# A two-layer conv / recurrence / pooling backbone: layer two's modulation as halves in the blockwise projection, and loads, casts and the norm's mean in another order

## The chip, the cores and the metric

The kernel runs on one core of one Trainium2 chip. Its time is device microseconds, lower is better. An instruction stream runs on each engine: PE (TensorE: matmuls; PEld is its weight load), DVE (VectorE), ACT (ScalarE), POOL (GpSimd) and SP (SyncE, which here only issues DMAs). Each takes its instructions in order and waits on semaphores for the others.

## The reference

One sequence of 1024 latent tokens with 1024 features (D), and 256 context tokens, pass two layers. Layer one (even) has a convolution branch and a recurrence branch side by side; layer two (odd) a pooling mixer.

```python
for l in range(2):
    shift, scale, gate = split(silu(c) @ mod_w[l] + mod_b[l], 3)
    h = rmsnorm(x, norm_g[l]) * (1 + scale) + shift
    if l == 0:
        va, vg, ga, xb, gb = split(h @ w_in, 5)
        u = depthwise_conv(va * sigmoid(vg), conv_w, conv_b)        # 31 taps
        y_a = silu(layernorm(u, ln_g, ln_b)) * silu(ga)
        y_b = rglru(shortconv(xb), h_ctx) * silu(gb)                # two directions, scan over tokens
        out = concat([y_a, y_b]) @ w_out
    else:
        u, g = split(h @ w_in2)                                     # 2048 each
        out = (einsum(pool(u), w_grp) * od_scale * silu(g)) @ w_out2
    x = x + gate * out
return rmsnorm(x, final_g)
```

The modulation of layer two (shift and scale, 16 columns of 128) needs only `c`, so it can be made at any time before layer two. Layer two's w_in and w_grp are multiplied beforehand in the kernel (the "folds").

## The kernel before

Features lie on the 128 partitions, tokens on the free axis, in row tiles of 128 and halves of 512 tokens. A float32 product is made of three matmuls: high part by high part, low by high, high by low. A weight is therefore loaded (wr), cast on ACT to its high part (wh) and subtracted on DVE or POOL to its low part (wl).

The stages in order:

1. Layer one's modulation, norm and two of the four folds, to about 104 us. Six whole rows of layer two's modulation are made here too (`mod_row_in`, L725).
2. A loop over eight feature tiles (xb, vg, va, then the recurrence's gates). DVE does the 31-tap convolution as a queue of small instructions; `fill(n)` issues the next n of them. For five tiles the sum of even and odd tokens is made ahead (`spread_sum`, into cL). The product gb follows, to about 520 us.
3. ga as four quads (`quad_fixed`: seven block products instead of eight, in banks qa, qb and qc), to 603.70 us. `cp_ga` copies a bank within a quad on ACT.
4. The blockwise projection of y_b, "wob": eight outputs of 48 matmuls (two halves of 24). Around it runs the layernorm of the convolution branch: `ln_mean` (matmul with ones), `ln_square` (subtract on DVE, square on ACT), `ln_add`, `ln_root` (matmul ms_ln of the sum lnsum, root on ACT), `ln_scale`, `ln_silu`, `ga_mult`. `wob_evict` takes a result out of PSUM by ACT (wo) and adds it on POOL (xp), or does both on DVE (m > 4). `raw_load`/`raw_split` bring a weight. `mod_half(0, n)` makes ten halves of modulation columns at m = 0.
5. The quads of y_a's projection, "woa", to about 795 us. Each product's bank is added to the residual tile x1 by DVE (L1498), and `mods` is stepped after each quad: the other ten halves. Then the two last folds run, to 839 us, and DVE scales x1 for layer two (L1547).
6. Layer two's quads v and g, pooling, the last projection and the final norm.

Up to the end of wob the order on every engine is the order of the program text: `on(engine, ...)` chains each instruction to the one before it. From there on a scheduler orders the instructions when the program is built. Every load goes through SP's queue, in its order, and waits there for a free buffer. Tiles of half width (lsq, wo, mod) share six buffers (`ttile`).

Of the kernel before, what the change touches and what calls it, by code (L numbers as in the profile page):

```python
# [49 lines left out]


NROW = 6
# [5 lines left out]
def body(ctx, tc, xT, ctxT, cc, ccol, modT, modW, win, gw, wout, wu, grp, wg, wo1, small, edge, ident, outT):  # L58
# [239 lines left out]
    rpool = tc.alloc_tile_pool(name="rpool", bufs=3)  # L298
# [3 lines left out]
    cL = cpool.tile([P, D], F32, name="cL")  # L302
    hh, hl, ch, cl = [], [], [], []
    with ExitStack() as sctx:
# [118 lines left out]
        def ctx_scale():  # L423
            rstd(accc, eps_r, "c")
            for i in range(2):
                v = cx[i].rearrange("p (k n) -> p k n", n=C)
                last["vec"] = nc.vector.tensor_tensor(out=v, in0=v, in1=accc.unsqueeze(1).to_broadcast([P, 4, C]),
                                                      op=mult)
# [45 lines left out]
        begin, chain[0] = chain[0], None  # L474
# [76 lines left out]

    def conv(j):
        acc_, late = banks(f"conv{j}", 0)
        ue, uo = us[j][:, 0::2], us[j][:, 1::2]
        ub = uo if j >= NSPREAD else both_sum(j)
# [3 lines left out]
        vec(nc.vector.tensor_scalar, out=acc_, in0=ue, scalar1=w(15), scalar2=None, op0=mult)  # L559
        yield  # L560
        vec(nc.vector.tensor_scalar, out=late, in0=uo, scalar1=w(16), scalar2=None, op0=mult)
        yield
        for n in range(NT + 1):
            if n < NT - 1 and n != 7:
                tap(acc_, ue, w(2 * n + 1), n - 7)
                yield
            if n != 8:
                tap(late, uo, w(2 * n), n - 8)
                yield
        if ub is uo:  # L570
# [23 lines left out]
    ended, summed, spread_ = [0], [1], [0]  # L594
    NSPREAD = 5

# [43 lines left out]
    with ExitStack() as actx:  # L640
# [91 lines left out]
        vec(nc.vector.tensor_tensor, out=m1[:, 0, :NROW], in0=m1[:, 0, :NROW], in1=col(O_MB + 3 * KT, NROW), op=add)  # L732
# [5 lines left out]
        for j in range(KT):  # L738
# [81 lines left out]
            fill(19 if state is None else 5 if final else 8)  # L820
# [54 lines left out]
        def gr_split(j):  # L875
            gws[j] = raw_split(grs.pop(j), f"gb{j}")
# [8 lines left out]
    rpool.release()  # L885
# [7 lines left out]
    m1p = hpool.tile([P, 2 * KT - NROW, 2], F32, name="m1p")  # L893
# [186 lines left out]
    def quad_weights(src, name):  # L1080
        raw = []
        for i in range(2):
            raw.append(wpool.tile([P, D], F32, tag="wr", name=f"wr_{name}_{i}"))
            sp(raw[i], src[i])
        a11, a12 = [raw[0][:, h] for h in HALF]
# [10 lines left out]

        yield op(a11, 1)
# [30 lines left out]
    def quad_fixed(name, keep, step):  # L1128
# [8 lines left out]
        for n, (ps, op, first) in enumerate(((a, "b11", True), (c, "t1", True), (b, "t2", False), (a, "b21", False),  # L1137
# [19 lines left out]
            pull()  # L1157
# [14 lines left out]

    def yr_step(n):
        if 0 < n < KT - 1:
            for h in range(2):
                yr_load(n + 1, h)
# [24 lines left out]
    block_sum(1)  # L1201
    gb_silu(4)
    gr_split(6)
    yr_step(1)
    block_split(1)
    gb_product(5, gws[5])
    block_sum(2)
    yr_step(2)
    block_split(2)
    block_sum(3)  # L1210
    gb_silu(5)
    gr_split(7)
    gb_product(6, gws[6])
    pull()
    yr_step(3)
# [3 lines left out]
    pull()  # L1219
# [27 lines left out]
    def mid_step(n):  # L1247
        fill(4)
# [7 lines left out]
    def wob_split(m):  # L1256
        if m < KT:
            gws[KT + m] = raw_split(obs.pop(m), f"wob{m}", vadd if m > 5 else gp)

    def last_step(n):  # L1260
# [11 lines left out]
        if n in (3, 5):  # L1272
            wob_split(n // 2 - 1)
            wob_load(n // 2 + 1)
# [10 lines left out]
    def xp_load(m, h):  # L1285
        if m < KT:
            xps[m, h] = vtile(f"xp{m}_{h}")
            sp(xps[m, h], xT[m][:, HALF[h]])

# [13 lines left out]

    lnmu, lnsq = {}, {}

    def ln_mean(h):
        lnmu[h], lnsq[h] = banks(f"mu{h}", h)
        on("pe", nc.tensor.matmul, lnmu[h], ones, lnacc[h][:, :H], start=True, stop=True)
# [748 lines left out]
```

## Time and profile before

| | us |
|---|---|
| median of 3 runs | 1334.56 (1333.38 to 1336.40) |
| profiled execution | 1333.44 |
| span of its instructions | 1331.6 |
| PE busy | 1274.4 (96%) |
| DVE busy | 1175.9 (88%) |
| ACT busy | 651.1 (49%) |
| POOL busy | 383.8 (29%) |
| mean granted clock of PE | 0.986 |

A row of the timeline gives start and duration in us, the engine, the line, output<-inputs and their shapes; in brackets the idle time before it and what ended it. Lines of the changed kernel are numbered differently from L725 on; helper calls all carry one line (L481 before, L477 after), so they are told apart by the names of tiles.

### The profile page before, as it was taken

The page shows a single profiled execution, that of the slowest core. Times are in us where ns is not written, and L with a number is a line of the kernel's source. Part 1 is how long each engine was busy: PE and PEld are TensorE (multiplying, and loading weights), DVE is VectorE, ACT ScalarE, POOL GpSimd, SP SyncE. Part 2 cuts the span into 40 slices and gives each one's busy share as a digit, 9 for nine tenths or more (in the row PEclk, how much of TensorE's full clock was granted, in tenths as well). Part 3 has the DMA queues.
Part 4 walks back from the last instruction along what each step waited for, and adds up shares of the span by engine and source line. Part 5 has one row for each costly group of instructions (what it writes and reads, how often), then busy time and mean ns, then how long its engine had stood idle before and what let it go on. Part 6 is the DMA issues. An engine that isn't in the chain of part 4 may idle for free. (4 is left out here: it accounts for less than half of the span.)

```text
span 1331.6 us, 15798 instructions
## 1 busy us (share of the span) xinstructions
PE 1274.4 (96%) x5552; PEld 1018.0 (76%) x5552; DVE 1175.9 (88%) x1780; ACT 651.1 (49%) x949; POOL 383.8 (29%) x207
## 2 busy tenths in 40 slices
PE   8989999999999999999699999999999999989995
PEld 3458888888888887777477877788778888778784
DVE  7988999999999998996999778998999987876875
ACT  5333656666656623353754336734333334634542
POOL 3064555675657615673320023000000000000002
PEclk9999999999999999999899999999999999999998
DMA  9975111121112174468466457244333334868613
GB/s 357 392 256 182 49 41 55 56 72 40 64 43 69 64 265 165 140 212 282 148 199 206 162 168 238 79 150 150 112 112 118 111 119 139 300 208 276 231 64 126
DMA packets 91218, 206.96 MB, mean 155 GB/s; under 512 B 8706, under 2 KB 28546, under 8 KB 91140
## 3 DMA queue, kind: packets, MB, share of 16 engines
q1 hardware_dynamic: 79236, 193.38, 42.8%
q10 hardware_dynamic: 11904, 12.59, 2.8%
q8 instruction: 43, 0.70, 0.2%
q14 instruction: 35, 0.29, 0.1%
HBM read 149.31 MB, written 56.62 MB: 155 GB/s over the span
## 5 line engine op out<-in xcount | busy, mean ns | idle before, releaser
L481 DVE SCALAR_TENSOR_TENSOR conv<-u,sm,conv 128x505 f32<-128x505 f32 (+6 forms) x224 | 152.6, 744 | 1.0
L1877 POOL TENSOR_TENSOR o<-x,rr 128x256 f32<-128x256 f32 (+1 forms) x9 | 8.0, 926 | 458.1 <-ACT rr L1865 455.2
L481 POOL TENSOR_TENSOR l<-l,l 128x1280 f32<-128x1280 f32 (+1 forms) x23 | 64.0, 2797 | 91.7 <-DVE l L481 65.5
L481 ACT ACTIVATE l<-g,sm 128x512 f32<-128x512 f32 (+1 forms) x96 | 58.6, 618 | 57.8 <-PE g L481 56.0
L285 PE MATMUL fold<-graw,wu 128*128 128x512 f32 x128 | 57.9, 613 | 2.7 <-DMA wu<-wu 2.7
L107 POOL TENSOR_TENSOR wl_wu<-wr_wu,wh_wu 128x1024 fp32r<-128x1024 f32 x8 | 19.3, 2410 | 122.4 <-ACT wh_wu L106 122.4
L481 PE MATMUL wob<-ybh,wl_wob 128*128 128x512 f32 x128 | 50.3, 393 | 1.7 <-POOL wl_wob L481 1.0
L481 PE MATMUL wob<-ybh,wh_wob 128*128 128x512 f32 x128 | 51.9, 405 | 0.0
L285 PEld LDWEIGHTS fold<-graw,wu 128*128 128x128 f32 x128 | 25.0, 197 | 34.9 <-issue 29.8
L481 PE MATMUL gb<-h0h,wl_gb 128*128 128x512 f32 x128 | 49.9, 390 | 1.5 <-POOL wl_gb L481 1.5
L106 ACT CAST wq_v<-wr_v 128x512 fp32r<-128x512 f32 x48 | 28.1, 620 | 46.2 <-DMA wr_v<-wfold 15.2
L481 PE MATMUL wob<-ybl,wh_wob 128*128 128x512 f32 x128 | 50.3, 393 | 0.0
L481 PE MATMUL vg<-h0h,wl_vg 128*128 128x512 f32 x128 | 50.0, 390 | 0.0
L481 PE MATMUL gb<-h0h,wh_gb 128*128 128x512 f32 x128 | 49.8, 389 | 0.0
L481 PE MATMUL gb<-h0l,wh_gb 128*128 128x512 f32 x128 | 49.8, 389 | 0.0
L481 PE MATMUL vg<-h0h,wh_vg 128*128 128x512 f32 x128 | 49.8, 389 | 0.0
L481 PE MATMUL vg<-h0l,wh_vg 128*128 128x512 f32 x128 | 49.8, 389 | 0.0
L481 PE MATMUL va<-h0h,wh_va 128*128 128x512 f32 x128 | 49.8, 389 | 0.0
L481 PE MATMUL va<-h0l,wh_va 128*128 128x512 f32 x128 | 49.8, 389 | 0.0
L481 PE MATMUL va<-h0h,wl_va 128*128 128x512 f32 x128 | 49.8, 389 | 0.0
L481 DVE TENSOR_TENSOR_SCAN l<-l,l 128x256 f32<-128x256 f32 (+1 forms) x32 | 48.7, 1521 | 1.1
L106 ACT CAST wq_g<-wr_g 128x512 fp32r<-128x512 f32 x48 | 28.3, 620 | 41.8 <-DVE wr_g L972 12.5
(697 smaller groups left out, 4393.6 us busy)
## 6 DMA issues: line engine op xcount, KB each, us to landing
mod<-modT SPq DMA_DIRECT2D x20, 512.0 KB, 7.4
x_part<-xp SPq DMA_DIRECT2D x32, 256.0 KB, 3.8
wr_v<-wfold SPq DMA_DIRECT2D x16, 512.0 KB, 4.0
wr_g<-wg SPq DMA_DIRECT2D x16, 512.0 KB, 4.7
wr_wo<-wo SPq DMA_DIRECT2D x16, 512.0 KB, 4.3
y_b<-y SPq DMA_DIRECT2D x24, 256.0 KB, 3.2
y_t<-y SPq DMA_DIRECT2D x24, 256.0 KB, 3.3
yr_t<-y_t SPq DMA_DIRECT2D x12, 512.0 KB, 5.9
```

Of the source, the lines that this page charges most:

```text
L106: return (nc.scalar.copy(hi, src), eng.tensor_tensor(out=lo, in0=src, in1=hi.bitcast(F32), op=sub))
L107: eng.tensor_tensor(out=lo, in0=src, in1=hi.bitcast(F32), op=sub))
L285: nc.tensor.matmul(ps, w[:, kc], gs[i], start=(i == 0), stop=(i == 3))
L481: last[eng] = f(*args, **kw)
L1877: nc.gpsimd.tensor_tensor(out=o[:, k - k0], in0=v, in1=rr, op=mult)
```

## The change

It has five parts.

- **Modulation of layer two.** The six whole rows at the start and the ten first halves at wob's m = 0 go away. All sixteen columns are made as two halves each in `mod_halves`, 32 steps, taken 4, 10, 9 and 9 after the four quads of woa (3, 3, 2 and 2 of ten steps before).
- **Convolution.** For the first six tiles two taps are computed on ACT (`conv_heads`), so that the first two DVE instructions add them in and two later taps fall away. The sums of `spread_sum` are made on POOL instead of DVE. `fill` counts change: 10 for 8 in the loop, 3 for 4 in the middle quads, none at wob's m = 0.
- **The layernorm in wob.** The convolution is ended before wob. The mean is taken after three of eight k-steps of output 0 instead of after output 0. Squares move from m = 1 to m = 0, roots to m = 1 and 2 (h = 0), scales and silus by one step.
- **Splits and loads.** gb's splits 5 to 7 go from POOL to DVE, wob's splits of 0, 1 and 5 too. Outputs' weights are loaded three ahead instead of four; the layer's x is loaded before the last quad ends.
- **Quads of ga.** `quad_weights` yields more often and is pulled by a table (1, 1, 1, 2, 1, 2, 1), so that instructions of the next quad's weights fall between others.

```diff
-        with tc.issue_after(begin.ins):
-            for n in range(NROW):
-                mod_row_in(rpool.tile([P, D], F32, tag="r", name=f"row{n}"), modT[1, n], m1[:, 0, n : n + 1])
...
+    def conv_heads(j):
+        for t, v, k in ((heads[0], us[j][:, 0::2], 17), (heads[1], us[j][:, 1::2], 18)):
+            act(t[:, : H - 1], v[:, 1:], AF.Identity, scale=col(O_CONVW + 31 * j + k))
+        headed[0] = j + 1
...
-        vec(nc.vector.tensor_tensor, out=cL[:, HALF[j % 2]], in0=us[j][:, 1::2], in1=us[j][:, 0::2], op=add)
+        gp(out=cL[:, HALF[j % 2]], in0=us[j][:, 1::2], in1=us[j][:, 0::2], op=add)
...
-            fill(19 if state is None else 5 if final else 8)
+            fill(19 if state is None else 5 if final else 10)
...
-            gws[j] = raw_split(grs.pop(j), f"gb{j}")
+            gws[j] = raw_split(grs.pop(j), f"gb{j}", vadd)
...
-            pull()
+            pull((1, 1, 1, 2, 1, 2, 1)[n])
...
-            gws[KT + m] = raw_split(obs.pop(m), f"wob{m}", vadd if m > 5 else gp)
+            gws[KT + m] = raw_split(obs.pop(m), f"wob{m}", gp if 1 < m < 5 else vadd)
...
     def mod_halves():
+        for n in range(2 * KT):
+            mod_half(0, n)
+            yield
         load_c(0, cH, HALF[1])
-        for n in range(NROW, 2 * KT):
+        for n in range(2 * KT):
...
         if m == 0:
-            for _ in range(KT - 1):
+            for k in range(KT - 1):
                 for h in range(2):
                     next(steps[h])
+                if k == 2:
+                    for h in range(2):
+                        ln_mean(h)
         for h in range(2):
             all_of(steps[h])
-            if m == MEAN + 1:
+            if m == 0:
                 for j in range(KT):
                     ln_square(j, h)
...
+            if h == 0 and m in (1, 2):
+                ln_root(m - 1)
+            if m == 2 and h == 0:
+                ln_scale(0)
...
-            if m == 0:
-                if h == 0:
-                    half_c(0)
-                for n in range(NROW + 5 * h, NROW + 5 * h + 5):
-                    mod_half(0, n)
         wob_split(m + 2)
-        wob_load(m + 4)
+        wob_load(m + 3)
...
-        for _ in range((3, 3, 2, 2)[m // 2]):
+        for _ in range((4, 10, 9, 9)[m // 2]):
             next(mods)
```

How the order on the engines changes is shown at three places. First ACT in ga, where the first quad ends and the second quad's weights begin (o00 a finished block, cp the copied bank, wq a weight's cast). Before:

```order
L481 ACTIVATE o00_ga0_4173<-qa_ga0_4086 128x512
L481 DMA ga_raw0_93<-o00_ga0_4173 128x512
L481 CAST wq_ga2q_1_4183<-wr_ga2q_0_4176 128x512
L481 COPY cp_ga0_4204<-qb_ga0_4088 128x512
L481 CAST wq_ga2q_5_4207<-wr_ga2q_1_4178 128x512
```

and now:

```order
L477 ACTIVATE o00_ga0_4183<-qa_ga0_4095 128x512
L477 DMA ga_raw0_93<-o00_ga0_4183 128x512
L477 COPY cp_ga0_4209<-qb_ga0_4097 128x512
L477 CAST wq_ga2q_1_4212<-wr_ga2q_0_4186 128x512
L477 CAST wq_ga2q_5_4236<-wr_ga2q_1_4188 128x512
```

The copy stands ahead of the first cast instead of behind it.

Second ACT in wob (lsq the squares by tile and half, wo an output taken out of PSUM by output and half, wh_wob the cast of an output's weights, sq_ln the root). Before:

```order
L481 ACTIVATE wo_0_1_4853<-wob0_1_4780,m0_176 128x512
L481 CAST wh_wob2_4876<-wr_wob2_4708 128x1024
L481 ACTIVATE mu0_1_4883<-u0_895 128x512
...
L481 ACTIVATE lsq7_1_5000<-u7_3258 128x512
L481 ACTIVATE wo_1_1_5003<-wob1_1_4888,m0_176 128x512
L481 CAST wh_wob3_5011<-wr_wob3_4748 128x1024
L481 ACT_TABLE_LOAD
L481 ACTIVATE sq_ln0_5048<-ms_ln0_0_5045,eps_l_139 128x512
```

and now:

```order
L477 ACTIVATE lsq6_1_4873<-u6_2923 128x512
L477 ACTIVATE lsq7_1_4877<-u7_3265 128x512
L477 ACTIVATE wo_0_1_4882<-wob0_1_4759,m0_176 128x512
L477 CAST wh_wob2_4892<-wr_wob2_4752 128x1024
L477 ACTIVATE wo_1_0_4924<-wob1_0_4898,m0_176 128x512
L477 ACT_TABLE_LOAD
L477 ACTIVATE sq_ln0_4933<-ms_ln0_0_4930,eps_l_139 128x512
```

The cast of output 2's weights stood ahead of the squares and now stands behind all sixteen.

Third DVE in the last quad of woa (x1_7 and x1_6 the residual tiles that take the banks qa, qb and qc; gl a low part for the folds; mod1_n_q half q of modulation column n). Before:

```order
L1498 SCALAR_TENSOR_TENSOR x1_7_6074<-qc_woa6_6076,m0_176,x1_7_6074 128x512
L1488 TENSOR_TENSOR n1acc0_5597<-n1acc0_5597,n1q6_0_0_6134 128x512
L540 SCALAR_TENSOR_TENSOR mod1_12_1_6063,m1p_3688<-mod1_12_1_6063,cH_3689 128x512
L540 SCALAR_TENSOR_TENSOR mod1_13_1_6068,m1p_3688<-mod1_13_1_6068,cH_3689 128x512
L540 SCALAR_TENSOR_TENSOR m1_178<-m1p_3688,sm_131 128x1
L1498 SCALAR_TENSOR_TENSOR x1_7_6074<-qb_woa6_6077,m0_176,x1_7_6074 128x512
```

and now:

```order
L1513 SCALAR_TENSOR_TENSOR x1_6_6062<-qc_woa6_6065,m0_176,x1_6_6062 128x512
L104 TENSOR_TENSOR gl_2_0_6251<-graw_2_0_6248,gh_2_0_6250 128x1024
L536 SCALAR_TENSOR_TENSOR mod1_0_1_6034,m1p_3696<-mod1_0_1_6034,cH_3697 128x512
L536 SCALAR_TENSOR_TENSOR mod1_1_1_6038,m1p_3696<-mod1_1_1_6038,cH_3697 128x512
L536 SCALAR_TENSOR_TENSOR mod1_2_1_6042,m1p_3696<-mod1_2_1_6042,cH_3697 128x512
L536 SCALAR_TENSOR_TENSOR mod1_3_1_6046,m1p_3696<-mod1_3_1_6046,cH_3697 128x512
L536 SCALAR_TENSOR_TENSOR mod1_4_1_6050,m1p_3696<-mod1_4_1_6050,cH_3697 128x512
L536 SCALAR_TENSOR_TENSOR mod1_5_1_6054,m1p_3696<-mod1_5_1_6054,cH_3697 128x512
L536 SCALAR_TENSOR_TENSOR m1_178<-m1p_3696,sm_131 128x1
L1513 SCALAR_TENSOR_TENSOR x1_7_6063<-qb_woa6_6066,m0_176,x1_7_6063 128x512
```

The last eviction but one of the quad's banks stood behind two halves of modulation and now stands behind six and a gl split.

More of the change, by code (lines that the diff above doesn't have):

```diff
@@ L302, in body @@
     cL = cpool.tile([P, D], F32, name="cL")
+    heads = [cpool.tile([P, H], F32, name=f"head{i}") for i in range(2)]
     hh, hl, ch, cl = [], [], [], []
@@ L554, in conv @@
         ue, uo = us[j][:, 0::2], us[j][:, 1::2]
+        ahead = j < NHEAD
+        if ahead and headed[0] <= j:
+            conv_heads(j)
         ub = uo if j >= NSPREAD else both_sum(j)
@@ L591, in conv @@
         ended[0] = j + 1
-    ended, summed, spread_ = [0], [1], [0]
+    ended, summed, spread_, headed = [0], [1], [0], [0]
     NSPREAD = 5
+    NHEAD = 6
+    for t in heads:
+        nc.vector.memset(t[:, H - 1 :], 0.0)
     def vadd(**kw):
@@ L1280, in body @@
         late.pop(0)()
-    xps, xouts = {}, []
[L1285 to L1288, printed above, removed]
+    while ended[0] < KT:
+        fill(1)
+    ln_sums()
     def wob_evict(m, h):
```

125 lines of the change are left out of this document (65 added, 60 removed).

## The prediction

> **What bounds the kernel now.** First the page's busy line and slices, then PE's waits by releaser, then the timelines at the longest of them.
>
> ```profile
> PE 1274.4 (96%) x5552; PEld 1018.0 (76%) x5552; DVE 1175.9 (88%) x1780; ACT 651.1 (49%) x949; POOL 383.8 (29%) x207
> PE ms_ln L481 <- DVE lnsum L481: 10.2, 2, 9.0
> PE qc_woa L994 <- DVE wq_woa L107: 2.0, 1, 2.0
> PE wob L481 <- DVE wl_wob L481: 0.8, 1, 0.8
> ```
>
> PE is busy for 1274.4 us of 1331.6, so time can only come from its 57 us of idle, or from a slower clock. The matmuls themselves stay the same. The largest single wait is 9.0 us of 10.2: the layernorm's sum of squares (ms_ln) waits for DVE. By stretches:
>
> ```profile
> 400.00:450.00 50.00, 50.00 (x227) 41.58 (x226) 48.27 (x58) 35.58 (x38) 38.42 (x16) 1.00 0.19 63
> 520.00:604.00 84.00, 79.20 (x338) 63.98 (x338) 83.06 (x121) 39.59 (x65) 57.36 (x41) 0.98 0.51 175
> 604.00:706.00 102.00, 90.02 (x378) 71.42 (x377) 87.51 (x127) 51.35 (x76) 25.78 (x15) 0.95 0.62 208
> 706.00:795.00 89.00, 84.78 (x369) 68.56 (x368) 74.02 (x130) 38.97 (x64) 6.00 (x3) 1.00 0.54 178
> 795.00:839.00 44.00, 43.42 (x196) 35.18 (x195) 36.80 (x60) 28.48 (x45) 13.29 (x6) 1.00 0.67 207
> ```
>
> The columns are length, busy PE, PEld, DVE, ACT, POOL, clock, DMA share, GB/s. In the loop (400 to 450) PE never idles, so DVE work saved there is worth nothing at once. The wob stage (604 to 706) loses 12 us of PE. The woa stage has PE idle for 4.2 us, and DVE has 15 us to spare.
>
> **The wob stage: old waits go, one new wait comes.** Why the 9 us wait exists:
>
> ```profile
> 603.70 0.39 PE L481 MATMUL wob<-ybh,wh_wob 128*128 128x512 f32 x1
> 605.97 0.39 PE L481 MATMUL wob<-ybl,wh_wob 128*128 128x512 f32 x1
> 619.32 0.69 DVE L481 SCALAR_TENSOR_TENSOR mod<-mod,cH 128x512 f32<-128x512 f32 x1 [8.66 <-ACT cH L481]
> 631.42 2.47 DVE L481 TENSOR_TENSOR u<-u,mu 128x512 f32<-128x512 f32 x4
> 641.15 0.68 DVE L481 TENSOR_TENSOR lnsum<-mu,lsq 128x512 f32<-128x512 f32 x1
> 648.44 0.69 DVE L481 TENSOR_TENSOR u<-u,mu 128x512 f32<-128x512 f32 x1
> 641.89 2.08 PE L481 MATMUL ms_ln<-lnsum,ones 128*128 128x512 f32 x2 [9.05 <-DVE lnsum L481]
> 642.98 1.42 PE L481 MATMUL wob<-ybh,wh_wob 128*128 128x512 f32 x1
> 644.62 0.63 PE L481 MATMUL wob<-ybh,wl_wob 128*128 128x512 f32 x1
> 651.58 1.13 PE L481 MATMUL ms_ln<-lnsum,ones 128*128 128x512 f32 x2 [1.20 <-DVE lnsum L481]
> 654.15 0.50 PE L481 MATMUL wob<-ybh,wl_wob 128*128 128x512 f32 x1 [0.97 <-POOL wl_wob L481]
> ```
>
> DVE waited 8.66 us for the conditioning half and ran ten modulation halves, so the subtractions began at 631.42, 27.7 us after the stage's first matmul (T0 = 603.70 here). The change takes those ten away and takes the mean after 18 of the 48 matmuls of the first output. Matmuls follow each other every 0.227 us (ten of them from 603.70 to 605.97), so the mean is there at T0 + 4.1 us. DVE still has the last splits to do, now with wl_wob of outputs 0 and 1 on it as well; I put its first subtraction at T0 + 6.2. From there the rows above repeat: the first sum is ready 10.4 us later (631.42 to 641.83), at T0 + 16.6, and the last half of the subtractions ends 17.7 us later, at T0 + 23.9. PE reaches ms_ln after 74 matmuls, at T0 + 16.8. Both waits of ms_ln (9.05 and 1.20) go.
>
> The same order delays something else. All sixteen squares now stand ahead of the cast of output 2's weights on ACT, where before they stood ahead of output 3's. How long weights take behind the squares is in the trace:
>
> ```profile
> 650.33 1.03 ACT L481 CAST wh_wob<-wr_wob 128x1024 fp32r<-128x1024 f32 x1
> 651.73 2.37 POOL L481 TENSOR_TENSOR wl_wob<-wr_wob,wh_wob 128x1024 fp32r<-128x1024 f32 x1
> ```
>
> From the last subtraction (649.13) to the first matmul that uses wl (654.15) are 5.0 us. So output 2's weights are whole at T0 + 28.9. PE, with nothing else to wait for, comes to output 2 after 99 matmuls, at T0 + 22.5. That is a **new wait of 6.4 us** (4.6 if DVE begins at the mean, 8.4 if it begins 2 us later). Everything on PE is queued behind it; the second ms_ln too. Before it, m = 3 cost 0.97 in the same way.
>
> A long gap also costs clock: after the 9.05 us wait the matmuls come every 0.43 us (644.19 to 645.89), and at full rate again by 646.1. Seven or eight of them at 0.2 us too much are 1.7 us. [...]
>
> Sum of the stage: minus 9.05, 1.20, 0.97, 0.76 and 1.7 (13.7 us), plus 6.4 and 1.7, plus 0.3 for outputs 4 and 5, whose casts now stand behind silus: **−5.3 us** (−11 to −2).
>
> **The ga and gb stage.**
>
> ```profile
> 509.27 0.50 PE L481 MATMUL gb<-h0h,wl_gb 128*128 128x512 f32 x1 [1.49 <-POOL wl_gb L481]
> 538.65 0.50 PE L481 MATMUL qb_ga<-hth,wq_ga0q 128*128 128x512 f32 x1 [2.34 <-ACT cp_ga L481]
> 537.49 0.62 ACT L481 CAST wq_ga2q<-wr_ga2q 128x512 fp32r<-128x512 f32 x1 [5.18 <-DMA wr_ga2q<-win]
> L481 DVE TENSOR_TENSOR wl_wob<-wr_wob,wh_wob x2: 1208/1211/1214, 686.6 to 693.2; 128x1024 fp32r<-128x1024 f32 x2
> 600.81 0.50 PE L481 MATMUL qb_ga<-hth,wq_ga6q 128*128 128x512 f32 x1 [1.04 <-ACT cp_ga L481]
> ```
>
> ACT sat 5.18 us on a weight load with PE's copy (cp_ga) queued behind; the copy now goes first. The last copy stood behind a wob cast and now does not. gb's last weights are split on DVE, where 128x1024 takes 1.21 us (wl_wob) against 2.4 on POOL. The three waits sum to 4.87; I take **−4.0**, since the copy still needs its own product and wob's casts crowd ACT (−5.5 to −1.5). The 1.38 us wait for wq_ga6q, which POOL makes as before, I leave.
>
> **The woa stage takes the modulation.** Twenty-two more halves are stepped here (32 against 10), 256 KB each, 5.8 MB in all, plus six combining instructions.
>
> ```profile
> L540 DVE SCALAR_TENSOR_TENSOR mod<-mod,cH x10: 679/687/2843, 743.5 to 803.4; 128x512 f32<-128x512 f32 x10
> mod<-modT SPq DMA_DIRECT2D x20, 256.0 KB, 4.8
> DMA to landing us min/median/max: 3.3/5.5/10.2
> 779.95 1.22 DVE L107 TENSOR_TENSOR gl<-graw,gh 128x1024 fp32r<-128x1024 f32 x1
> 784.82 2.84 DVE L540 SCALAR_TENSOR_TENSOR mod<-mod,cH 128x512 f32<-128x512 f32 x1 [1.79 <-DMA mod<-modT]
> 784.73 2.39 POOL L107 TENSOR_TENSOR wl_wu<-wr_wu,wh_wu 128x1024 fp32r<-128x1024 f32 x1 [105.25 <-ACT wh_wu L106]
> 790.45 0.74 DVE L1498 SCALAR_TENSOR_TENSOR x<-qb_woa,m,x 128x512 f32<-128x512 f32 x1
> 791.24 0.50 PE L991 MATMUL qb_woa<-ya_t4h,wq_woa 128*128 128x512 f32 x1 [1.73 <-DVE x L1498]
> ```
>
> 22 × 0.69 is 15.2 us of DVE, as much as it has to spare. What PE feels is where they stand. The qb bank of a quad is used by three products, and each must be evicted (x) by DVE before the next starts; 791.24 shows PE waiting on that. In the last quad the eviction now stands behind one gl split (1.22) and six halves (6 × 0.62 = 3.7) that come after the qc eviction. qc's product ends 2.7 us before qb's, so PE would wait 0.7 + 1.2 + 3.7 + 0.7 + 0.1 − 2.7 = 3.7 us. In the third quad ten halves pass through a pool of six buffers with 4.8 us from issue to landing. The seventh to tenth land only 4.8 us after the first four are used, and the eviction behind them comes about 2.5 us late. The first two quads cost 0 to 1.5. That is 6.2 us. The old waits of this stage (1.99 and 1.73, 3.7 us) go: DVE comes to woa with its norm done some 15 us earlier relative to PE, and no wl_wu stands in the way at the last eviction. Net **+2.5** (−2 to +8).
>
> Then v0: the last halves' loads are queued on SP behind the last store of woa, and the identity for rs must follow the last half into the same buffer (3.6 us, issue at 804.08 to use at 807.73).
>
> ```profile
> 793.87 0.39 PE L994 MATMUL qb_woa<-ya_t4h,wq_woa 128*128 128x512 f32 x1
> 803.35 0.69 DVE L540 SCALAR_TENSOR_TENSOR mod<-mod,cH 128x512 f32<-128x512 f32 x1
> 807.73 0.69 DVE L208 TENSOR_TENSOR dg_n<-cH,rc_n 128x512 f32<-128x512 f32 x1 [0.44 <-DMA cH<-ident]
> 811.45 4.03 DVE L1547 SCALAR_TENSOR_TENSOR x<-x,a,ms_n 128x512 f32<-128x512 f32 x6
> ```
>
> Before, the last half ended 9.9 us after woa's last matmul (794.1); now nine halves are left at that point, three of them waiting for buffers, and I get about 13.5. The identity then arrives 3.5 us later, but 13 fold matmuls (3 us) that used to run ahead of woa's end now run behind it and cover that. **+0.8** (0 to +5).
>
> **Start and loop.**
>
> ```profile
> L481 DVE SCALAR_TENSOR_TENSOR row<-row,cL x6: 1218/1316/1468, 86.3 to 95.3; 128x1024 f32<-128x1024 f32 x6
> ```
>
> Six rows of 1.3 us and their 3 MB leave the start, and one 2.4 us POOL split moves ahead of the context's: 0 (−2 to +2.5). In the loop five sums leave DVE and about two instructions in each of six convolutions, while more fills are called per pass, so the queue is as long; the sums become 1.3 us POOL work. 0, covered by PE's 50.00 of 50.00; without that cover the difference would be 17 × 0.69 = 12 us of DVE.
>
> [...]
>
> **Sum.** −5.3 − 4.0 + 2.5 + 0.8 = −6.0. The profiled execution took 1333.44 (span 1331.6 and 1.8 around it), which gives 1327.4; the median of the runs lies 1.1 above it, so **1328.5**.
>
> **Rivals.**
> First, the new wait does not come, because ACT gets to output 2's cast early or DVE starts at the mean: the wob stage then gives 12 in place of 5.3, and the whole −12.7: 1321.9. For it: 20.8 us of DVE idle (619.32 less 8.66, to 631.42) and modulation are gone. Against: sixteen squares really stand ahead of the cast. Chance 0.22.
> Second, the other side: the modulation in woa decides. If halves land as late as the slow ones (10.2 us, the longest of all tiles of that name in the rows above) and each is held by a POOL instruction as at 784.82, the third and fourth quads wait 6 and 8 us, and v0 is late by 5 as its scaling (811.45) follows the last half. Woa and v0 then cost 6 + 8 + 5 − 3.7 = +15.3 instead of +3.3, and the sum is +6: 1340.5. It decides from 9 us of waiting in these places. For it: DVE's margin is all used. Against: DMA at 0.54 has room. Chance 0.13.
> Third, about no change: the wob wait is 8.4 us and woa costs 4 more, or the part that looks sooner is not (the norm's sum still waits for DVE's earlier splits): −6.0 + 2 + 4 = 0: 1334.5. Chance 0.15.
>
> My forecast has 0.50. Within 0.2% (2.7 us) is about what a measurement can't tell from no change: faster 0.72, same 0.15, slower 0.13. The forecast's own bounds give 1323 to 1332; with the rivals 1318 to 1338 leaves 0.2 out.
>
> **What would show it.** No wait of ms_ln for lnsum over 1.5 us; a wait of wob for wl_wob, 4.5 to 8 us long, at the third output, with a clock near 0.9 in its slice; no wait for cp_ga; waits of qb_woa for x of 2 to 4 us in the third and fourth quads; DVE's x scaling 17 to 21 us after woa's last matmul. Wrong if the wob wait is absent, or if waits of over 9 us in all stand in woa and before v0.

## The result and the profile after

The changed kernel takes 1384.23 us in the median (1378.76 to 1386.53), the kernel before 1333.97 beside it (1332.4 to 1336.4). The ratio is 1.0369, 95% interval 1.0335 to 1.0404: it is slower by 50 us. I had forecast 1328.5, in a range of 1318 to 1338; the result lies far outside it, on the side of the second rival, and the largest part of it stands where I had written 0.

The first matmul of each stage on PE gives the stages' lengths. The profiled execution of after spans 1384.7 us, that of before 1331.6:

| stage (us) | before | after | difference | my term |
|---|---|---|---|---|
| start, to vg | 104.6 | 94.1 | −10.5 | 0 |
| loop, vg to gb | 319.8 | 350.6 | +30.8 | 0 |
| gb and ga | 179.3 | 192.6 | +13.3 | −4.0 |
| wob | 105.6 | 98.2 | −7.4 | −5.3 |
| woa and folds | 129.9 | 146.8 | +16.9 | +2.5 |
| v0 to the first g | 15.3 | 23.7 | +8.4 | +0.8 |
| the rest | 477.1 | 478.7 | +1.6 | 0 |

The page's busy line of after, and PE's longest waits by releaser (total, times, longest; left out are three waits, one in the start and two in the rest):

```profile
PE 1298.0 (94%) x5552; PEld 1029.6 (74%) x5552; DVE 1183.3 (85%) x1788; ACT 658.6 (48%) x961; POOL 386.2 (28%) x206
PE vg L477 <- POOL wl_vg L477: 8.3, 3, 4.4
PE g L477 <- DVE u L477: 6.6, 4, 3.0
PE qb_woa L997 <- DVE m L536: 4.7, 1, 4.7
PE qa_woa L1000 <- DVE wq_woa L104: 4.6, 1, 4.6
...
PE gb L477 <- POOL wl_gb L477: 4.4, 1, 4.4
...
PE qb_woa L997 <- ACT qb_woa L1013: 3.3, 1, 3.3
PE g L477 <- ACT l L477: 3.0, 2, 1.6
PE qb_woa L997 <- DVE x L1513: 2.8, 1, 2.8
PE qa_ga L477 <- ACT sb L477: 2.7, 1, 2.7
PE qa_ga L477 <- POOL wq_ga4q L477: 2.7, 1, 2.7
```

The old list was led by ms_ln (10.2 us) and had nothing from the loop. Now ms_ln and cp_ga are gone, as forecast, and the loop leads: vg and g wait there, and gb right behind it. The same in stretches (length, busy PE, PEld, DVE, ACT, POOL, clock, DMA share, GB/s):

```profile
250.00:300.00 50.00, 43.07 (x188) 34.62 (x188) 49.44 (x65) 29.84 (x34) 32.88 (x16) 0.97 0.19 64
350.00:400.00 50.00, 43.99 (x186) 36.16 (x186) 49.47 (x62) 24.70 (x29) 24.78 (x11) 0.90 0.15 48
637.00:735.00 98.00, 93.43 (x392) 74.21 (x392) 83.11 (x110) 51.75 (x76) 35.90 (x13) 0.98 0.51 169
735.00:833.00 98.00, 82.50 (x337) 66.20 (x336) 77.00 (x142) 36.63 (x62) 3.10 (x1) 0.93 0.62 210
```

In the loop PE's row was 50.00 of 50.00 before. Now PE idles 6 to 7 us of 50 in these two windows and the clock is 0.90 to 0.97. DVE is full there (49.4), but it was nearly so before: in the six windows of 50 us from 125 to 425 us its row of before is 46.5 to 49.5. Over the whole loop PE is busy for 332.9 us of 350.6, against 319.8 of 319.8: of the +30.8 us, 17.7 are waits and 13.1 matmuls that take longer. In woa PE idles 15.5 us of 98.

What happened on DVE in the loop is seen at the first two instructions of a convolution. The timeline of after around them, on DVE, POOL and ACT:

```profile
225.54 6.33 POOL L477 TENSOR_TENSOR l<-l,uc 128x1280 f32<-128x1280 f32 x2
225.74 6.68 DVE L477 SCALAR_TENSOR_TENSOR conv<-u,sm,head 128x512 f32<-128x512 f32 x2 [1.71 <-ACT head L477]
...
339.50 2.63 ACT L477 ACTIVATE l<-l,tiny 128x1280 f32<-128x1280 f32 x2
342.03 1.39 ACT L477 ACTIVATE head<-u,sm 128x511 f32<-128x511 f32 x2
341.01 6.32 POOL L477 TENSOR_TENSOR l<-l,l 128x1280 f32<-128x1280 f32 x2 [3.54 <-ACT l L477]
342.80 5.08 DVE L477 SCALAR_TENSOR_TENSOR conv<-u,sm,head 128x512 f32<-128x512 f32 x2 [9.26 <-ACT head L477]
```

Two things are to be seen. DVE waits for `head`, which stands in ACT's queue behind the recurrence's activations (9.26 us at 342.80, 1.71 at 225.74). And the two instructions themselves take 6.68 and 5.08 us in place of 1.4: at 225.74 they end with POOL's two products, 0.6 us behind them. These two instructions read `u` and `head`, both in SBUF; an ordinary tap reads its running sum from PSUM.

How a late DVE makes PE wait for vg is seen at the longest of those waits. The recurrence's scans on DVE end at 272.2; POOL's product `l` waits for them, and vg's low part stands behind it:

```profile
272.24 2.36 POOL L477 TENSOR_TENSOR l<-l,l 128x1024 f32<-128x1024 f32 x1 [11.64 <-DVE l L477]
274.55 2.37 POOL L477 TENSOR_TENSOR wl_vg<-wr_vg,wh_vg 128x1024 fp32r<-128x1024 f32 x1
276.98 0.78 PE L477 MATMUL vg<-h0h,wl_vg 128*128 128x512 f32 x1 [4.37 <-POOL wl_vg L477]
```

### The profile page after: what moved, and what is told of

Same layout as the page of the kernel before. It is cut to its first block, busy times and chain, and to the rows that moved or that the text cites. A ratio compares the mean times of both kernels' runs of the same rounds, so it can differ in the third digit from the quotient of the medians.

```text
span 1384.7 us, 15818 instructions
## 1 busy us (share of the span) xinstructions
PE 1298.0 (94%) x5552; PEld 1029.6 (74%) x5552; DVE 1183.3 (85%) x1788; ACT 658.6 (48%) x961; POOL 386.2 (28%) x206
## 4 chain that ended last, share of the span: by engine, by line
PE 43%; DVE 21%; DMA 14%; issue 8%; ACT 7%; POOL 5%; SPq 1%; ACTq 0%; POOLq 0%; DVEq 0%
DVE conv L477 6%; PE fold L282 4%; PE vg L477 4%; PE xb L477 3%; PE gb L477 2%; PE g L477 2%; DMA wr_g<-wg 2%; PE va L477 2%; DMA x_part<-xp 1%; DVE l L477 1%; POOL xp L477 1%; DMA wr_wo<-wo 1%; DVE ws L1609 1%; DMA wr_wu<-wu 1%; DMA mod<-modT 1%
## 5 line engine op out<-in xcount | busy, mean ns | idle before, releaser
L477 DVE SCALAR_TENSOR_TENSOR conv<-u,sm,conv 128x506 f32<-128x506 f32 (+6 forms) x212 | 144.3, 746 | 0.9
L103 ACT CAST wq_g<-wr_g 128x512 fp32r<-128x512 f32 x48 | 28.3, 622 | 46.5 <-DMA wr_g<-wg 15.4
```

The costliest lines, as they stand in the source:

```text
L103: return (nc.scalar.copy(hi, src), eng.tensor_tensor(out=lo, in0=src, in1=hi.bitcast(F32), op=sub))
L477: last[eng] = f(*args, **kw)
```

## Experiments

All lengths below are of profiled executions, by the same first matmuls; "total" is a kernel's time. Beside the first four kernels before took 1332.73 us, beside the next four 1335.2, beside the last four 1333.13 and 1332.66. The first eight kernels were run once each, the last four 4 to 10 times; their total is the median, and the profiled run lies up to 3 us from it. From gb on single profiles spread: "loop undone" and "no modulation" are the same program up to the end of wob and have 182.8 and 179.4 us in gb and ga, and the rest, which no edit touches, is 476.1 to 482.0. A difference of less than some 4 us there shows nothing by itself.

| kernel | start | loop | gb, ga | wob | woa, folds | v0 to g | rest | total |
|---|---|---|---|---|---|---|---|---|
| before | 104.6 | 319.8 | 179.3 | 105.6 | 129.9 | 15.3 | 477.1 | 1333.97 |
| after | 94.1 | 350.6 | 192.6 | 98.2 | 146.8 | 23.7 | 478.7 | 1384.23 |
| no heads | 93.2 | 322.3 | 186.8 | 100.4 | 148.5 | 24.0 | 480.7 | 1357.72 |
| eight fills | 94.1 | 329.1 | 186.7 | 100.2 | 146.6 | 21.5 | 480.0 | 1359.99 |
| heads still | 94.2 | 336.9 | 190.9 | 97.1 | 145.8 | 23.5 | 479.3 | 1369.48 |
| heads, one input | 93.5 | 338.4 | 190.3 | 98.2 | 146.8 | 22.5 | 479.7 | 1371.16 |
| loop undone | 93.1 | 322.6 | 182.8 | 99.6 | 145.7 | 24.7 | 476.8 | 1347.09 |
| no modulation | 93.9 | 322.6 | 179.4 | 98.1 | 133.8 | 15.9 | 480.3 | 1325.78 |
| four ahead | 94.0 | 322.6 | 180.4 | 104.2 | 137.2 | 23.3 | 480.8 | 1344.49 |
| spread | 94.3 | 322.7 | 181.6 | 108.9 | 138.7 | 18.2 | 476.3 | 1342.59 |
| eight in wob | 94.8 | 322.6 | 183.1 | 99.6 | 145.5 | 22.4 | 482.0 | 1349.73 |
| eight late | 94.2 | 322.6 | 178.9 | 100.4 | 144.4 | 21.8 | 477.7 | 1341.81 |
| rows back | 103.9 | 319.8 | 180.7 | 103.6 | 136.8 | 16.0 | 476.1 | 1337.87 |
| three rows | 101.4 | 319.8 | 180.7 | 100.0 | 135.1 | 24.6 | 478.1 | 1344.75 |

### The loop: heads or fills?

Two theories: the heads on ACT make DVE late, or the ten fills a pass for eight do. "No heads" takes the first away, "eight fills" the second.

```diff
-    NHEAD = 6
+    NHEAD = 0
```

> The convolution's two ACT terms are taken out (no tile has them); the fills of 10 and the sums on POOL stay. Heads theory (the loop's 28 us come from DVE's two convolution instructions that read an ACT-made tile, which wait for ACT and are held by POOL): the loop from the first vg to gb goes back from 345 us to about 320, and the whole to 1345 to 1360. Fills theory (two more fills per pass overload DVE): the loop stays at 340 or grows, since each convolution now has two instructions more; the whole stays near 1380. Sums theory (POOL's sums stand ahead of the vg weights): the loop stays at about 345.

```diff
-            fill(19 if state is None else 5 if final else 10)
+            fill(19 if state is None else 5 if final else 8)
```

> Only the fills at the loop's tail go back from 10 to 8; heads and sums on POOL stay. Fills theory: the loop comes back to about 322 us and the whole to 1350. Heads theory: the loop stays above 335, as the heads are still waited for and held; with 12 instructions fewer in the loop at most 8 us go.

Without heads the loop is 322.3, 28.3 us shorter, with ten fills and POOL's sums still in it. With heads and eight fills it is 329.1: 21.5 of the 30.8 us go as well, which neither theory had said. So it is neither alone but the two together. Ten fills without heads (322.3) cost nothing against eight without heads (322.6, in the kernel "loop undone" below, which also has the sums back on DVE), heads with eight fills cost 6.5, and both 28.0. I read it so: with ten fills the queue of taps is ahead, and a convolution begins at a point of the pass at which ACT and POOL are in the middle of the recurrence. DVE's waits for `head` between 195 and 425 us are 11.0 us with ten fills and 3.0 with eight, and the twelve instructions that read `head` take 1.70 us in the median with ten and 0.76 with eight. "No heads" at the place of 225.74 (DVE, POOL, then DVE's next taps):

```profile
223.28 1.40 DVE L477 TENSOR_SCALAR conv<-u,sm 128x512 f32<-128x512 f32 x2
223.38 5.91 POOL L477 TENSOR_TENSOR l<-l,uc 128x1280 f32<-128x1280 f32 x2
224.59 2.04 DVE L477 SCALAR_TENSOR_TENSOR conv<-u,sm,conv 128x505 f32<-128x505 f32 x3
```

POOL runs the same two products at the same time, and DVE's two instructions take 1.40 us, not 6.68: they have one SBUF input each. The three taps behind them, with their running sum in PSUM, aren't held either (2.04).

### The heads: wait or hold?

"Heads still" leaves the two ACT instructions out and adds a constant tile instead. DVE then has nothing to wait for and still reads two SBUF inputs.

```diff
-            act(t[:, : H - 1], v[:, 1:], AF.Identity, scale=col(O_CONVW + 31 * j + k))
+            pass
...
-        nc.vector.memset(t[:, H - 1 :], 0.0)
+        nc.vector.memset(t, 0.0)
```

> ACT does not compute the two terms; DVE reads the same tiles, which hold zeros from the start (the output lacks two of 31 taps in six feature tiles). So there is nothing to wait for, and the second operand still lies in SBUF. If the hold by POOL is what costs (the two instructions take 3.5 to 6.7 us instead of 1.4), durations over 2 us stay and the loop keeps about half of its loss, 10 to 15 us. If the wait for ACT is what costs, the loop is back at 320 us.

"Heads, one input" keeps ACT's heads and the wait for them, but the DVE instruction reads the head alone.

```diff
-                vec(nc.vector.scalar_tensor_tensor, out=acc, in0=v, scalar=w(k), in1=t, op0=mult, op1=add)
+                vec(nc.vector.tensor_scalar, out=acc, in0=t, scalar1=w(k), scalar2=None, op0=mult)
```

> ACT computes the two terms and DVE waits for them, but its two instructions read only the head tile (one operand in SBUF; the output lacks two of 31 taps in six feature tiles). If the hold needs a second SBUF operand, the two instructions take 0.7 us each whenever they start, and only the wait for ACT remains: 10 to 15 us of the loop's loss. If the wait alone explains the loss, the loop stays at 345.

DVE's timeline at the third convolution, of "heads still" and then, at the third and fifth, of "heads, one input":

```profile
223.78 5.56 DVE L477 SCALAR_TENSOR_TENSOR conv<-u,sm,head 128x512 f32<-128x512 f32 x2
```

```profile
224.68 1.41 DVE L477 TENSOR_SCALAR conv<-head,sm 128x512 f32<-128x512 f32 x2 [1.76 <-ACT head L477]
336.55 1.42 DVE L477 TENSOR_SCALAR conv<-head,sm 128x512 f32<-128x512 f32 x2 [9.86 <-ACT head L477]
```

The two causes come apart cleanly. Without the wait the hold stays (5.56 us), and the loop is 14.6 us above the one without heads (336.9 − 322.3). With one input the hold is gone (1.41, 1.42) and the wait stays (9.86), and the loop is 16.1 above it (338.4). Both together cost 28.3, so the two (30.7) nearly add up. Both theories' sizes of 10 to 15 us were a little low for the second.

The same two instructions take 5.56 us with two SBUF inputs, 1.41 with one and 1.40 without the heads.

### The whole loop part undone

"Loop undone" sets heads to none, fills to eight, the sums back to DVE and the middle quads' fills to four; the rest of the change stays.

```diff
-    NHEAD = 6
+    NHEAD = 0
-        gp(out=cL[:, HALF[j % 2]], in0=us[j][:, 1::2], in1=us[j][:, 0::2], op=add)
+        vec(nc.vector.tensor_tensor, out=cL[:, HALF[j % 2]], in0=us[j][:, 1::2], in1=us[j][:, 0::2], op=add)
-            fill(19 if state is None else 5 if final else 10)
+            fill(19 if state is None else 5 if final else 8)
-        fill(3)
+        fill(4)
```

> The whole loop part of the change is undone (no head taps, eight fills a pass, all sums on DVE, the first mid step's four fills as before); loads, casts, the norm's mean and the modulation stay as in the change. If the loop's +30.8 us and the lateness of gb and ga (+13.3) both come from the loop's edits, the loop takes about 320 us, gb and ga together about 180 (before 179.3), and the whole about 1350. If GpSimd's sums have no part and the fills neither, the loop is as with the heads alone undone (322.3) and the whole 1356 to 1358. The late stages should not move in either case: woa with its folds about 147, the step from v0 to g about 23.

The loop is 322.6, as with the heads alone undone, so without heads neither the sums on POOL nor the ten fills cost anything there. No kernel has the heads with the sums on DVE; at 272.24 POOL waits for DVE's scans, and not behind a sum. Gb and ga come to 182.8: of their +13.3 us, 5.8 went with the heads (192.6 to 186.8), 4.0 with sums and fills (to 182.8), and 3.5 are left; the last two lie within the spread. The total is 1347.09 with before at 1335.2: the rest of the change, which I had put at −6, is slower by itself, by 12 us. The late stages stand unchanged, as expected (145.7 and 24.7).

### The modulation in woa, or late weights?

"No modulation" leaves out the 32 halves and their loads and uses constants for the columns. "Four ahead" loads wob's weights four ahead again, with all halves where the change has them. Both start from "loop undone".

```diff
     def mod_halves():
-        for n in range(2 * KT):
-            mod_half(0, n)
+        nc.vector.memset(m1[:, :, : 2 * KT], 0.1)
+        nc.vector.memset(a1, 1.0)
+        for n in range(64):
             yield
```

> As the kernel with the loop undone, and the 32 halves of layer two's modulation and their loads are left out (the combined values are constants, so the output differs there). If the halves' place in the woa stage is what costs the late stages, woa with its folds falls from about 147 to 126-132 us and the step from v0 to g from about 23 to 14-17: 23-28 us less in all. If instead the weight loads that are issued three ahead cost it, the waits at woa's start (4.6 and 3.3 us) stay, woa only falls to about 138, and the whole falls by 12 to 15 us.

```diff
             wob_split(1)
             wob_load(2)
+            wob_load(3)
...
-        wob_load(m + 3)
+        wob_load(m + 4)
```

> As the kernel with the loop undone, but wob's weights are loaded four ahead as before the change. If the loads' order makes woa's first weights late, the waits at woa's start (4.6 for wq_woa, 3.3 for qb) go and the whole is 6 to 9 us below the kernel with the loop undone. If what holds SP's queue is the store of x behind GpSimd's 18 us product, moving one load ahead of it only moves the others: the waits stay within 2 us of those and the whole too.

Without the halves woa with its folds falls by 11.9 us, the step to g by 8.8, the total by 21.3, to 1325.78. That is a little less than the first theory gave (23 to 28) and more than the second (12 to 15). The waits at woa's start stay (2.9 and 3.3 us), as the second had it, so they have another cause. Where they come from is seen in after, on POOL and DVE, SP and then PE:

```profile
679.75 1.29 POOL L477 TENSOR_TENSOR xp<-xp,wo 128x512 f32<-128x512 f32 x1 [5.03 <-ACT wo L477]
699.32 18.02 POOL L477 TENSOR_TENSOR xp<-xp,wo 128x512 f32<-128x512 f32 x2 [3.91 <-ACT wo L477]
...
714.39 0.76 DVE L1321 SCALAR_TENSOR_TENSOR xp<-wob,m,xp 128x512 f32<-128x512 f32 x1
```

```profile
715.67 0.33 SPq L477 DMA_DIRECT2D x_part<-xp  x1
716.04 0.43 SPq L477 DMA_DIRECT2D wr_wob<-wout  x1
...
722.78 0.52 SPq L963 DMA_DIRECT2D wr_woa<-wout  x1
```

```profile
740.72 0.50 PE L1000 MATMUL qa_woa<-ya_b11h,wq_woa 128*128 128x512 f32 x1 [4.62 <-DVE wq_woa L104]
750.93 0.50 PE L997 MATMUL qb_woa<-ya_t2h,wq_woa 128*128 128x512 f32 x1 [3.31 <-ACT qb_woa L1013]
```

A POOL product that takes 1.29 us alone takes 18.02 for two, and the first of them 16.3, while DVE streams some 25 instructions with two SBUF inputs between 699 and 714. The store of x stands behind it in SP's queue, and wob's last load and woa's first ones behind the store.

In "four ahead" the 3.8 and 2.3 us that these two waits have in "loop undone" are both gone, and woa is 8.5 us shorter. That the order of the loads did this is not shown, for the hold of 18 us is gone there too. Beside the same stream of DVE, POOL's two products take 1.40 and 1.70 us, and DVE's pairs are the ones that are held:

```profile
659.61 2.38 DVE L477 TENSOR_TENSOR u<-u,gat 128x512 f32<-128x512 f32 x2
660.04 1.40 POOL L477 TENSOR_TENSOR xp<-xp,wo 128x512 f32<-128x512 f32 x1 [3.91 <-ACT wo L477]
662.61 1.70 POOL L477 TENSOR_TENSOR xp<-xp,wo 128x512 f32<-128x512 f32 x1 [1.18 <-ACT wo L477]
```

Two pairs of DVE take 2.38 and 2.35 us there in place of 1.28. The split of wob's sixth weights stands behind them, and PE's wait for it grows from 1.7 to 3.9 us; wob is 4.6 longer in all. The total is 2.6 lower and not the 6 to 9 of the first theory, but single runs do not resolve 2.6.

### Another place for the halves?

Three kernels look for a place in which the halves cost less; all have the loop undone, four loads ahead, and the identity in a buffer of its own. "Spread" has sixteen in wob and four behind each quad of woa. "Eight in wob" has eight and then 8, 8, 8 and 0, "eight late" eight and then 8, 6, 6, 4.

```diff
+            if m == 2 and h == 1:
+                half_c(0)
+            if m > 3:
+                mod_next(2 * (m - 4) + h)      # multiplies two halves, loads the next two
...
-        for _ in range((4, 10, 9, 9)[m // 2]):
+        for _ in range((4, 4, 4, 4)[m // 2]):
             next(mods)
-    idD = cH[:, :P]
+    idD = ttile('idT')[:, :P]
```

> Loop undone, loads four ahead, and the modulation's sixteen first halves go into the wob stage (two in each slot from the fifth output, each loaded one slot ahead), the second halves four in each quad of woa, the identity into its own buffer. If the halves' place in woa costs 16.9 us and the step from v0 to g 8.4, woa with its folds comes to 132-138 us, the step to 15-19 and wob to 100-106, the whole to 1322-1336. If VectorE simply has no room for 32 halves anywhere between wob and v0, wob grows to over 110 and the whole stays above 1340.

```diff
+            if 3 < m < 7 and 2 * (m - 4) + h < 5:
+                mod_next(2 * (m - 4) + h)
...
-        for _ in range((4, 10, 9, 9)[m // 2]):
+        for _ in range((8, 8, 8, 0)[m // 2]):   # "eight late": (8, 6, 6, 4)
```

> Loop undone, loads four ahead; eight of the 32 halves in wob's fifth to seventh outputs (loaded one slot ahead, so that woa's weights are not queued behind many of them), the other 24 behind the evictions of woa's first three quads (8, 8, 8 and none behind the fourth), the identity in its own buffer. Theory that the place of the halves costs the time: the 9.7 and 6.5 us waits for woa's weights go, the step from v0 to g comes to 15-18 us, woa with its folds to 130-136, wob to 103-107, the whole to 1322-1332. Theory that VectorE's total work between wob and v0 is what counts (22 us of halves, wherever they stand): the sum of wob, woa with folds and the step stays at 262-266 us as in the kernel with four loads ahead (264.7) and in the spread one (265.8), the whole at 1338-1343.

> As the kernel with eight halves in wob, but 8, 6, 6 and 4 halves behind woa's four quads, so that four halves stand behind the last eviction and ahead of v0's scaling. If halves behind the last eviction are what makes v0 late, the step from v0 to g is 2-4 us longer than with 8, 8, 8 and none, and waits of qb for m or x in the second and third quads are shorter by 1-3 us in all: the whole within 2 us of the other. If the place between the quads does not matter, both steps are the same.

None finds one. In "spread" woa's first weights were issued behind the halves' loads, and PE waits 9.7 and 6.5 us for them; its step to g is shorter (18.2), as I read it because woa is late. "Eight in wob" and "eight late" take those waits away (one of 3.7 us for qb stays at woa's start), and the time comes back elsewhere: ratio to before 1.0118 (1.0079 to 1.0156) and 1.0063 (1.0040 to 1.0087). Four halves behind the last eviction or none make the step to g 21.8 and 22.4 us: my reading that these four make v0 late is not borne out. The two differ by 7.9 us in the median all the same; in the profiles 8.5 of 10.0 us lie in gb and ga and in the rest, where their programs are alike. So the 7.9 us are not shown to come from the halves' place.

From wob's first matmul to g's first, the whole stretch in which the halves can stand, the windows say it (before, after, loop undone, no modulation, one row each):

```profile
603.70:854.50 250.80, 233.94 (x1007) 187.87 (x1006) 213.59 (x338) 130.13 (x204) 45.78 (x29) 0.98 0.59 192
```

```profile
637.30:906.00 268.70, 243.21 (x1008) 193.23 (x1007) 223.13 (x369) 130.31 (x205) 56.59 (x27) 0.96 0.58 189
```

```profile
598.50:868.50 270.00, 245.81 (x1007) 194.38 (x1006) 223.63 (x371) 130.28 (x205) 56.35 (x27) 0.94 0.58 190
```

```profile
595.90:843.70 247.80, 235.17 (x1008) 189.22 (x1008) 197.38 (x283) 130.12 (x204) 57.68 (x27) 0.99 0.52 172
```

With 32 halves the stretch is 264.7 to 272.9 us in the ten kernels that have them, with four different places for them, with none 247.8. Between "loop undone" and "no modulation" it is 22.2 us, and DVE's busy time there differs by 26.3. Half of what PE loses is no wait in the list but slower matmuls: 1007 of them are busy for 243.21 us in after and 233.94 in before (9.3 of 17.9 us).

### The rest of the change without its modulation

"Rows back" has the modulation as before the change (six rows at the start, ten halves in wob, ten in woa as 3, 3, 2, 2), the ten in wob behind the norm. "Three rows" has three at the start, eight halves in wob, eighteen in woa (5, 5, 5, 3). Both also drop the tiles of the heads.

```diff
+NROW = 6                                     # "three rows": 3
...
+        with tc.issue_after(begin.ins):
+            for n in range(NROW):
+                mod_row_in(rpool.tile([P, D], F32, tag="r", name=f"row{n}"), modT[1, n], m1[:, 0, n : n + 1])
...
-        for _ in range((4, 10, 9, 9)[m // 2]):
+        for _ in range((3, 3, 2, 2)[m // 2]):  # "three rows": (5, 5, 5, 3)
```

> The change with its loop part undone, loads four ahead, and the modulation spread as before the change: six whole rows at the start, ten halves in wob (here at its fifth to seventh outputs, behind the norm), ten halves behind woa's quads (3, 3, 2, 2). What is left of the change is the sooner mean, the moved copies and casts and the identity's own buffer. If the rows' removal is what made the start 10.5 us shorter, vg's first matmul is back at 103-106 us. If my terms for wob (-5.3) and for ga and gb (-4.0) hold by themselves and woa costs nothing new, woa with its folds is 127-132, the step from v0 to g 15-17, wob 98-103, and the whole 1321-1329. If VectorE's place for the ten halves in wob costs as much as the old wait of the norm did, wob stays at 104-108 and the whole is 1330-1336.

> As the kernel with the rows back, but three rows at the start, eight halves in wob and eighteen behind woa's quads (5, 5, 5, 3). A row at the start costs 1.75 us by the 10.5 us for six; a half behind woa's quads about 0.7-1 us once VectorE's spare time there is used. If the price is per instruction, the start is 5 us shorter than with six rows, woa with its folds and the step 5-8 us longer, and the whole within 3 us of the other. If woa and the step jump instead (by over 10 us), the price has a point from which it decides, between ten and eighteen halves.

The start is back at 103.9, so the rows were its 10.5 us. The group of DVE between 50 and 105 us says what they were (busy, mean ns, then the idle time before them; "rows back" has the same 7.8, and 2.2 idle):

```profile
L481 DVE SCALAR_TENSOR_TENSOR row<-row,cL 128x1024 f32<-128x1024 f32 x6 | 7.8, 1332 | 2.5 <-DMA row<-modT 2.5
```

7.8 busy and 2.5 idle are 10.3 us. The loop is 319.8 to the tenth. (The 2.8 us that it had more in "loop undone" went with the rows or with the heads' tiles; these two were not separated.)

With the rows back and the ten halves of wob in this later place, what is left of the change is a little slower than before too: 1337.87, ratio 1.0034 (1.0014 to 1.0053). So the second theory of "rows back" has the total nearly (1330 to 1336 expected), for another reason: wob is 103.6, 2.0 us better than before, gb and ga are 1.4 worse, woa 6.9 worse. PE's waits there:

```profile
PE wob L481 <- DVE wl_wob L481: 4.7, 2, 3.9
...
PE qc_woa L1009 <- DVE wq_woa L106: 3.6, 1, 3.6
```

The norm no longer waits, and the waits stand at the end of wob and the start of woa. I take it that DVE meets them with the work that it did not do earlier; no run parts that from POOL's turn, which makes the 3.9 us in "four ahead" (POOL's two products take 1.38 and 1.75 us here too). "Three rows" is 1344.75, 1.0081 (1.0052 to 1.0109). Its start is 2.5 us shorter, not 5, and woa with the step 6.9 longer: the first number speaks against a price for each row, the second lies within the expected 5 to 8. The whole, expected within 3 us, is 6.9 longer in the median and 2.8 in the profiles. The jump over 10 us did not come. No kernel of this study that computes the whole result beats before.

## Why the prediction was wrong, point by point

**The loop: the step that failed.** "So DVE work saved there is worth nothing at once" was read from PE's full row, and I made it the answer for the edit as a whole ("0, covered by PE's 50.00 of 50.00"). The row of the same window gave DVE 48.27 of 50. PE's full row covers what DVE does less; it does not cover a DVE that gets later, and DVE had 0.5 to 3.5 us in 50 to give. I counted the instructions that leave DVE and did not price the wait on ACT that the two new ones bring, nor what stands ahead of `head` in ACT's queue. What the runs put in its place is +30.8 us: 16.1 by the wait with the hold gone, 14.6 by the hold with the wait gone, and both together only with ten fills (28.0, against 6.5 with eight). A row of before had shown a DVE instruction that ran long beside POOL, the half at 784.82 with 2.84 us beside 2.39, and I priced none of that in the loop: the five sums on POOL cost nothing there without heads, the heads cost the hold.

**The start.** 0 was forecast, −10.5 came. The group row of before gives it: six rows on DVE ahead of vg, 7.8 busy and 2.5 idle. I had the first of these numbers and took it for hidden work, without naming anything that hides it.

**gb and ga.** −4.0 was forecast, and +13.3 came. With the loop undone the eight kernels have −0.4 to +3.8, "loop undone" itself +3.5, so the spread leaves the sign open, but −4.0 came in none. The two waits of cp_ga did go; the one of gb is 4.4 us in after and goes only with the loop undone. In "loop undone" new ones stand in their place, for sb 2.0 and for wq_ga0q, 2q and 4q 1.1, 1.6 and 1.9, 6.6 us together, where the old three were 4.87. I had priced where the copy went and not where the weights' instructions of each quad went.

**wob.** −5.3 was forecast and −7.4 came. The old waits of the norm went and the new one came, as described. PE of after, output 2 of wob, with the stage's first matmul at T0 = 637.3:

```profile
662.98 0.50 PE L477 MATMUL wob<-ybh,wh_wob 128*128 128x512 f32 x1 [0.77 <-ACT wh_wob L477]
665.71 0.50 PE L477 MATMUL wob<-ybh,wl_wob 128*128 128x512 f32 x1 [1.99 <-POOL wl_wob L477]
```

The first subtraction began at T0 + 5.7 (T0 + 6.2 forecast), the second matmul above at T0 + 28.4 (28.9): DVE's and the weights' times are right to half a microsecond. PE's is not: it came to output 2 at T0 + 24.9, not at T0 + 22.5, so the wait is 2.8 us in all (0.77 and 1.99) and not 6.4. The sum's second 1.7, for slower matmuls behind a wait of 6.4 us, was my assumption, and no run shows it; what after shows, behind the 0.77 and 1.99, is ten matmul starts from 665.71 to 669.69 that take 3.98 us, where 0.227 each would be 2.27. A wait of 1.7 for the sixth weights, where I had put 0.3, took part of that back. But the stage's gain is no gain of the kernel: from wob to g the stretch is 17.9 us longer.

**woa.** The two waits that I worked out came nearly as priced: the last quad 4.73 us for 3.7, the third 2.84 for 2.5.

```profile
807.58 0.50 PE L997 MATMUL qb_woa<-ya_t4h,wq_woa 128*128 128x512 f32 x1 [2.84 <-DVE x L1513]
828.92 0.76 PE L997 MATMUL qb_woa<-ya_t4h,wq_woa 128*128 128x512 f32 x1 [4.73 <-DVE m L536]
```

What I missed are 7.9 us at the stage's start (4.62 and 3.31), by loads that came late behind a held store (whether their new place in SP's queue has a part in it stays open), and matmuls that take longer: woa's and the folds' 550 are busy for 130.3 us, before for 125.1. That makes +16.9 for +2.5.

**v0.** DVE of after behind woa's last matmul, which ended at 834.0:

```profile
842.77 0.68 DVE L536 SCALAR_TENSOR_TENSOR mod<-mod,cH 128x512 f32<-128x512 f32 x1
843.62 0.69 DVE L536 SCALAR_TENSOR_TENSOR mod<-mod,cH 128x512 f32<-128x512 f32 x1
...
847.29 2.83 DVE L536 SCALAR_TENSOR_TENSOR mod<-mod,cH 128x512 f32<-128x512 f32 x1
...
857.92 4.69 DVE L1562 SCALAR_TENSOR_TENSOR x<-x,a,ms_n 128x512 f32<-128x512 f32 x7
```

The last halves ended 17 us after it, not 13.5, and the scaling began 24 us after it, where I had said 17 to 21. Two halves stand 0.85 us apart, not 0.69: the accumulator's read and the combining instruction come with each, and one half took 2.83 us beside a POOL instruction of 2.52 (from 847.05). With that the second rival was right in kind (the modulation decides, "DVE's margin is all used"): "loop undone", which has the modulation and none of the loop's edits, is at 1347.09, where that rival gave 1340.5. I had given it 0.13.

**What held:** no wait of ms_ln, none for cp_ga. The wait for wob's weights at the third output came, but with 2.8 us where I had said 4.5 to 8, and the waits of qb in the third and fourth quads with 2.84 and 4.73, where I had said 2 to 4. What I named as making the forecast wrong, over 9 us of waits in woa and before v0, happened.

## What to carry to other kernels

A full row of PE hid what another engine did less, but not what it did later: for each added wait, read the busy share of the waiting engine in that window, and where that is nearly full (46.5 to 49.5 of 50) price the wait in full (here 16 us from an edit that saves instructions). Work that is moved to another stage is paid where it lands, and idle time there is not yet room for it: from wob to g "no modulation" leaves DVE idle for 50 us of 247.8, and the halves' 26.3 us of DVE made the stretch 22.2 longer. Compare the length of the whole stretch, since a stage by itself showed −7.4 us while the stretch grew by 17.9. Before moving adds to another engine, look at where the operands lie: beside POOL's products three taps with their running sum in PSUM took 2.04 us ("no heads"), two that read `u` and `head` from SBUF 6.68 (after).

## What the hardware showed beyond what I expected

Two DVE instructions with two SBUF inputs took 6.68 us instead of 1.4 behind two POOL products, and the same two with one input 1.41.

The other direction was larger: of two POOL products of 1.29 us each, one took 16.3 us while DVE ran a stream of two-input instructions. The wait was not one DVE instruction (0.7 us) but the whole stream: the first instruction after it that takes an input from PSUM is the one at 714.39, and the product's store was issued 1.28 us behind it. In "eight in wob" DVE's stream breaks off after 8.6 us, and the product takes 9.8. It need not be POOL that is held: beside the same stream in "four ahead" POOL's products took 1.40 and 1.70 us, and DVE gave 2.2 us in their place. All seven kernels with loads three ahead have the pair at 18.0 to 18.5 us, those with four ahead at 3.1 or 11.0; what decides which of the two is held is not shown.
